# A two-block network on one core: the gates of the second block one stage later, through DRAM, and the experts' end in another order

## The chip, the core and the metric

The kernel runs on one core of a Trainium2 chip. The time is device microseconds of one execution, as the median of several runs. TensorE (PE) does the matrix products, VectorE (DVE), ScalarE (ACT) and GpSimd (POOL) work on elements, and SyncE (SP) issues nearly all loads of weights. Each engine runs its own instructions in order and waits on semaphores for the others.

## The reference

256 tokens of width 1024 pass a first block and then a second one of two layers, all in float32.

```
mod = silu(c) @ ada_w + ada_b                       # first block: 6 vectors of 1024
x = x + g_m * (mixer(norm(x) * (1+sc_m) + sh_m) @ w_out)     # RWKV-7 and mLSTM heads
x = x + g_f * hier_moe(norm(x) * (1+sc_f) + sh_f)            # 32 experts, 2 per token
x = rms_norm(x, final_norm_w)
for layer in 0, 1:                                  # second block
    shift, scale, gate = silu(c_2) @ ada_w_2[layer, 0] + ada_b_2[layer, 0]
    h = norm(x) * (1+scale) + shift
    y = hybrid_attention(h) if layer == 0 else pool_mixer(h)   # pool_mixer ends in * pool_scale
    x = x + gate * y
    shift, scale, gate = silu(c_2) @ ada_w_2[layer, 1] + ada_b_2[layer, 1]
    h = norm(x) * (1+scale) + shift
    x = x + gate * (square(relu(h @ mlp_w1[layer])) @ mlp_w2[layer])
return rms_norm(x, final_norm_w_2)
```

Each expert computes `(silu(x @ w_gate) * (x @ w_up)) @ w_down` with 1024 x 256 weights (256 x 1024 for down), 3 MB per expert. Shift and scale of one of the four sub-blocks of the second block take 8 MB of `ada_w_2`, its gate 4 MB.

## The kernel before

**Weights.** All weights are streamed once, 284 MB in all. SP loads them in pieces of 1 MB into eight slots named `w` (`slot`). For most products ACT casts a piece to a rounded high part `wh` (L293) and DVE subtracts it to get the low part `wl` (L294); the activations are split likewise, and each product is made of three matmuls: high with high, high with low, low with high. The helper `mm` records all of these at L180. Working tiles of 128 x 1024 (`t4`) come from a shared pool of 25; a tile can be taken only when its last user is done. PSUM has seven banks for general use and one for the modulation sums (`pada`).

**Modulation.** The vectors of shift, scale and gate are matrix-vector products whose weights are as large as those of the layers, so they are spread over the whole kernel as side work. There are two lists of side work: list 0 with pieces of products, list 1 with the modulations (`later`). `fill` and `more` take steps from them, `need` finishes one that is due, and the MLP takes up to four steps of list 1 in each of its groups. A step of `ada_steps` loads 1 MB and adds it up on TensorE with eight recorded matmuls (L454). A step of `vector_sum` loads 1 MB and adds it up on DVE in two instructions of 128 x 1024 (L532, L534); after eight steps four matmuls against ones add up over the partitions. `ada_cols` then turns the sums into columns (a DVE copy at L499, four transposes, adds at L505).

**The four gates of the second block.** The two gates of layer 0 are one item (`gates20`), summed together in eight steps during the first block's mixer, and kept as columns. `ada_gate` (by `rows_of`) turns one half of the columns into a row in all partitions: eight matmuls into `pgate` and two ACT copies, once in the attention and once ahead of the first MLP. The two gates of layer 1 are one item too (`gate_rows`), summed in the first MLP, written to DRAM by POOL, and read back into all partitions by two loads on SP each (`gate_load`).

**Order of list 1 in the first block.** `g1`, `f` (its own modulation), `ada00` (shift and scale of the attention), `gates20`, `ada01` (shift and scale of the first MLP). What is left is taken up in the attention.

**Experts.** The loop over `g` takes eight groups of four experts. `quad` multiplies the gathered slots of the four experts by the gate weights and then by the up weights (`pgu`), `act` makes the activation, `down` transposes it (`paT`, L1841), multiplies by the down weights (`pyd`), scales (`mg`, L1856) and splits the result, and `combine` of the group before adds it into `pacc` behind the next gate quad. `behind` holds the instructions of a part until the given instruction is issued. The loads of the expert weights follow in the order of use, as slots come free (`moe_done`). The residual is added to `pacc` as a product with a diagonal matrix (`residual`, `diag`), all eight matmuls at g = 7 ahead of the last `down`.

**Attention bias.** `attn_consts` builds a table of biases. Its last part loads the flipped rows from DRAM (`bflip`, POOL's queue), turns them by two matmuls per tile (`pbf`) and copies them to `bias`; it runs at g = 3 and g = 4. The attention's first weights are queued in `attn_first`, and `warm(W2)` puts six matmuls without use there.

**MLP and wide products.** In `wide_steps`, the first product of the MLP, a piece is used for four output blocks; for each block the high part's products are followed by the low part's.

Of the kernel before, what the change touches and what calls it, by code (L numbers as in the profile page):

```python
# [9 lines left out]
F32 = mybir.dt.float32  # L10
# [9 lines left out]
T = 256  # L20
# [41 lines left out]
W2 = 6  # L62
# [90 lines left out]
class Net:  # L153
# [392 lines left out]
    def gate_rows(self, l, out):  # L546

        nc, I = self.nc, self.I
        p = yield from self.vector_sum(1, [I["ada_w_2"][l, s][:, 2048:3072] for s in range(2)])
        t = self.t4("grow")  # L550
        s, f = t[:, 0:512], t[:, 512:1024]
        for j in range(4):
            nc.gpsimd.dma_start(s[32 * j:32 * j + 32],
                              I["ada_b_2"][l, j // 2:j // 2 + 1, 2048 + 512 * (j % 2):2560 + 512 * (j % 2)].to_broadcast([32, 512]))
        nc.vector.tensor_add(s, s, p)
        if l == 1:
            for j in range(2):
                nc.gpsimd.dma_start(f[32 * j:32 * j + 32], I["pool_scale_2"][:, 512 * j:512 * j + 512].to_broadcast([32, 512]))
            nc.vector.tensor_mul(s[0:64], s[0:64], f[0:64])
        d = out["d"] = self.dpool.tile([4, 512], F32, name=f"gate_d{l}")  # L560
        for j in range(4):
            nc.gpsimd.dma_start(d[j:j + 1], s[32 * j:32 * j + 1])

    def gate_load(self, d, half, name):
        g = self.t4(name)
        for j in range(2):
            r = 2 * half + j
            self.nc.sync.dma_start(g[:, j * 512:(j + 1) * 512], d[r:r + 1].to_broadcast([128, 512]))
# [198 lines left out]
    def wide_steps(self, H, wide, first, evac):  # L767
# [6 lines left out]
        for _ in range(4):  # L774
            for kc, h, l in self.piece():
# [10 lines left out]
                for j in range(4):  # L786
# [4 lines left out]
                    else:  # L791
                        mm(j, h, hh, 0, f)
                        mm(j, h, hl, 1, False)
                    mm(j, l, hh, 0, False)
# [898 lines left out]
    def overflow(self, S, gate, acc):  # L1693
# [5 lines left out]
        with tc.If(fl != 0):  # L1699
            co = mp.tile([128, 2, 32], F32, name="cwo", tag="cwo", bufs=1)  # L1700
            nc.vector.scalar_tensor_tensor(co, pos, CAP - 0.5, cw, op0=ALU.is_gt, op1=ALU.mult)
            cd = self.dpool.tile([32, 128, 2], F32, name="cwo_d")
            nc.gpsimd.dma_start(cd.rearrange("e p a -> p a e"), co, allow_slow_non_contiguous=True)
# [11 lines left out]
            with tc.For_i(0, 32, 1) as e:  # L1715
# [11 lines left out]
                cc = mp.tile([128, 1, 2], F32, name="ccol", tag="occ", bufs=1)  # L1727
                nc.gpsimd.dma_start(cc, cd[bass.ds(e, 1)].rearrange("o p a -> p o a"))
                for a in range(2):
# [10 lines left out]
                    nc.vector.tensor_scalar(act, act, cc[:, 0, a:a + 1], None, op0=ALU.mult)  # L1740
# [76 lines left out]
    def moe(self, S, consts):  # L1817
# [52 lines left out]
        def residual():  # L1870

            d = self.t4("diag")[:, 0:T]
            for a in range(2):
                da = d[:, a * 128:(a + 1) * 128]
                nc.vector.tensor_scalar(da, self.c("ident"), S["sd"][:, a:a + 1], None, op0=ALU.mult)
                for c in range(2):
# [782 lines left out]
```

## Time and profile before

| what | value |
|---|---|
| runs | 1039.04, 1031.16, 1039.94 us, median 1039.04 |
| profiled execution | 1031.61 us, its span 1029.9 |
| mean granted clock of TensorE | 0.978 |
| busy, share of the span | PE 92%, PEld 70%, DVE 56%, ACT 42%, POOL 4% |
| moved | 284.49 MB, mean 276 GB/s |
| instructions | 17630 |

The busy share of an engine is an average over stages that differ much: the first block's mixer lies before 290 us, the experts between 290 and 510, the attention up to 640, the first MLP up to 826, then the pool mixer and the second MLP. A time next to an instruction is its start, counted from the start of the span.

### The profile page before, as it was taken

How to read it: one execution, taken by the hardware profiler on the slowest of the kernel's cores; microseconds unless marked ns; L12 is line 12 of the kernel's file. 1: busy time of each engine (PE TensorE's matmuls, PEld its weight loads, DVE VectorE, ACT ScalarE, POOL GpSimd, SP SyncE). 2: the span in 40 equal slices, each digit the busy share in tenths (PEclk: the TensorE clock that was granted, in tenths of full speed). 3: DMA queues.
4: the chain of work that ended last, by engine and by line, in shares of the span. 5: the costliest groups of instructions: out<-in, count | busy, mean ns of one | idle time of the engine just before them, and what ended most of it. 6: DMA issues, size and time to landing. Idle time of an engine off the chain costs nothing. (4 is left out here: it accounts for less than half of the span.)

```text
span 1029.9 us, 17630 instructions
## 1 busy us (share of the span) xinstructions
PE 948.0 (92%) x7303; PEld 725.8 (70%) x7303; DVE 577.7 (56%) x987; ACT 435.1 (42%) x733; POOL 40.3 (4%) x55
## 2 busy tenths in 40 slices
PE   4899999999998788776989999999999989999996
PEld 2687776687665444433377798988888878888885
DVE  1475744657633221111266648998889776555556
ACT  1373223244332111111257545755555567555663
POOL 1011000010100000000000010010000000000000
PEclk9999999999899999988999999999999999999999
DMA  8989746997789999999977334699989935555501
GB/s 256 342 296 373 287 165 209 346 404 260 260 322 384 411 405 416 416 402 418 381 274 249 107 103 164 242 383 328 345 304 370 331 114 190 185 198 192 176 1 41
DMA packets 88760, 284.49 MB, mean 276 GB/s; under 512 B 10525, under 2 KB 13906, under 8 KB 76774
## 3 DMA queue, kind: packets, MB, share of 16 engines
q1 hardware_dynamic: 86922, 280.31, 73.7%
q0 software_dynamic: 800, 1.57, 0.6%
q10 hardware_dynamic: 956, 1.47, 0.4%
q8 instruction: 58, 0.95, 0.4%
q14 instruction: 24, 0.20, 0.1%
HBM read 282.25 MB, written 1.07 MB: 275 GB/s over the span
## 5 line engine op out<-in xcount | busy, mean ns | idle before, releaser
L180 PE MATMUL pB<-hx,wh 128*128 128x256 f32 (+1 forms) x1222 | 292.3, 323 | 3.1 <-ACT wh L293 1.5
L294 DVE TENSOR_TENSOR wl<-w,wh 128x1024 fp32r<-128x1024 f32 x186 | 225.5, 1221 | 121.5 <-ACT wh L293 118.9
L293 ACT CAST wh<-w 128x1024 fp32r<-128x1024 f32 x186 | 193.8, 1049 | 193.6 <-PE pB L180 101.9
L180 PEld LDWEIGHTS pB<-hx,wh 128*128 128x128 f32 x1222 | 200.6, 190 | 36.1 <-issue 10.7
L180 PE MATMUL pB<-hx,wl 128*128 128x256 f32 x800 | 221.3, 284 | 2.0 <-DVE wl L294 1.9
L180 PEld LDWEIGHTS pB<-hx,wl 128*128 128x128 f32 x800 | 149.9, 190 | 7.2 <-DVE wl L294 3.5
L180 PE MATMUL pgu<-w,xg 128*32 128x256 f32 x848 | 74.4, 439 | 29.7 <-DMA w<-in_moe_w_gate_dram 24.1
L180 PE MATMUL pm<-wh,fh 128*128 128x512 f32 (+1 forms) x262 | 100.9, 388 | 0.0
L180 PE MATMUL pm<-wl,fh 128*128 128x512 f32 (+1 forms) x262 | 100.9, 385 | 0.0
L180 PE MATMUL pm<-wh,fl 128*128 128x512 f32 (+1 forms) x262 | 100.9, 385 | 0.0
L180 PEld LDWEIGHTS pgu<-w,xg 128*32 128x32 f32 x848 | 33.3, 125 | 66.5 <-DMA w<-in_moe_w_gate_dram 32.6
L534 DVE SCALAR_TENSOR_TENSOR w<-w,csil 128x1024 f32<-128x1024 f32 x56 | 70.6, 1286 | 5.2 <-DMA w<-in_ada_w_dram 5.2
L180 PEld LDWEIGHTS pm<-wh,fh 128*128 128x128 f32 x262 | 49.2, 188 | 12.3 <-issue 2.5
L180 PEld LDWEIGHTS pm<-wh,fl 128*128 128x128 f32 x262 | 49.2, 188 | 10.0
L180 PEld LDWEIGHTS pm<-wl,fh 128*128 128x128 f32 x262 | 49.3, 188 | 9.7 <-DVE wl L294 0.4
L1856 DVE SCALAR_TENSOR_TENSOR mg<-pyd,slotw,g_f 128x512 f32<-128x512 f32 x16 | 12.0, 749 | 50.5 <-PE pyd L180 50.5
L1649 DVE TENSOR_TENSOR oh<-cs,pos 128x256 f32<-128x256 f32 x8 | 3.4, 426 | 65.0 <-PE pcw L180 64.9
L454 PE MATMUL pada<-w,csil 128*32 128x512 f32 x256 | 38.3, 603 | 0.0
L180 PE MATMUL pyd<-w,aT 128*32 128x512 f32 x216 | 30.5, 596 | 7.8 <-ACT aT L1843 7.8
L1678 ACT CAST slotT<-pcw 128x256 fp32r<-128x256 f32 x8 | 3.0, 373 | 80.0 <-PE pcw L180 80.0
L180 PEld LDWEIGHTS pxg<-oh,xp 128*128 128x128 f32 x256 | 29.2, 192 | 3.0 <-issue 2.5
L180 PE MATMUL pxg<-oh,xp 128*128 128x128 f32 x256 | 30.6, 278 | 0.1
(547 smaller groups left out, 1287.8 us busy)
## 6 DMA issues: line engine op xcount, KB each, us to landing
w<-in_mlp_w_dram SPq DMA_DIRECT2D x64, 1024.0 KB
w<-in_ada_w_dram SPq DMA_DIRECT2D x40, 1024.0 KB
w<-in_ada_w_dram SPq DMA_DIRECT2D x64, 512.0 KB
w<-in_moe_w_up_dram SPq DMA_DIRECT2D x28, 1024.0 KB
w<-in_moe_w_down_dram SPq DMA_DIRECT2D x26, 1024.0 KB
w<-in_moe_w_gate_dram SPq DMA_DIRECT2D x25, 1024.0 KB
w<-in_w_in_dram SPq DMA_DIRECT2D x12, 1024.0 KB
w<-in_attn_w_in_dram SPq DMA_DIRECT2D x9, 1024.0 KB
```

Source lines behind the costliest of these rows:

```text
L180: return self.nc.tensor.matmul(out, lhsT, rhs, **kw)
L293: nc.scalar.copy(h, w)
L294: self.split_ins = nc.vector.tensor_sub(l, w, h)
L454: nc.tensor.matmul(acc[32 * j:32 * j + 32, :], self.csil[:, which, k:k + 1].to_broadcast([128, 32]), w[:, j * 512:(j + 1) * 512], start=(k ...
L534: nc.vector.scalar_tensor_tensor(acc[:, s], w[:, s], ck, acc[:, s], op0=ALU.mult, op1=ALU.add)
L1649: nc.vector.tensor_tensor(oh.rearrange("p a (e s) -> p a e s", s=32), self.c("slots")[:, None, None, :].to_broadcast([128, 2, 4, 32]), S[" ...
L1678: nc.scalar.copy(ot, p[:, 0:T])
L1856: nc.vector.scalar_tensor_tensor(yg[:, s], py[c], cwg, gate[:, s], op0=ALU.mult, op1=ALU.mult)
```

## The change

1. The gates of the second block are four items `g00`, `g01`, `g10`, `g11`. Each sums one gate alone (`gate_row`, four loads of 1 MB that hold two parts each, two matmuls against ones), adds the bias, and writes two rows to DRAM by POOL. `gate_load` reads them back on SP. `g00` stands in the place of `gates20`; `g10` and `g01` are summed in the first MLP, `g11` in the second. `pool_scale` goes into `g10` alone.
2. `ada01` joins list 1 only after `route`; two steps of list 1 are taken ahead of the last `combine`.
3. The residual is added in halves, at g = 5 and g = 6, behind the gate quad. The loads of `bflip` move to SP's queue at g = 7; their products and copies come behind `attn_first`, and `W2` is 2.
4. In `wide_steps` the low part's products of all four blocks follow the high part's.
5. In the path for overflowing experts (a branch that isn't taken with these inputs) a table in DRAM has another layout.

```diff
-    def gate_rows(self, l, out):
+    def gate_row(self, l, h, out):
-        p = yield from self.vector_sum(1, [I["ada_w_2"][l, s][:, 2048:3072] for s in range(2)])
+        v = I["ada_w_2"][l, h][:, 2048:3072].rearrange("(p j) n -> p j n", j=8)
+        acc = None
+        for k in range(0, 8, 2):
+            w = self.slot()
+            nc.sync.dma_start(w.rearrange("p (j n) -> p j n", j=2), v[:, k:k + 2])
+            self.small_loads()
+            self.used(False)
+            for j in range(2):
+                x, ck = w[:, j * 1024:(j + 1) * 1024], self.csil[:, 1, k + j:k + j + 1]
+                if acc is None:
+                    acc = x
+                    nc.vector.tensor_scalar(acc, x, ck, None, op0=ALU.mult)
+                else:
+                    nc.vector.scalar_tensor_tensor(acc, x, ck, acc, op0=ALU.mult, op1=ALU.add)
+            yield 2.9
+        p = self.ps("pada", "ada")
         t = self.t4("grow")
+        s, f = t[0:64, 0:512], t[0:64, 512:1024]
+        for j in range(2):
+            q = slice(32 * j, 32 * j + 32)
+            self.mm(p[q], self.ones[:, 0:32], acc[:, j * 512:(j + 1) * 512], start=True, stop=True)
+            nc.gpsimd.dma_start(s[q], I["ada_b_2"][l, h:h + 1, 2048 + 512 * j:2560 + 512 * j].to_broadcast([32, 512]))
+        nc.vector.tensor_add(s, s, p[0:64])
...
+        d = out["d"] = self.dpool.tile([2, 512], F32, name=f"gate_d{l}{h}")
+        for j in range(2):
             nc.gpsimd.dma_start(d[j:j + 1], s[32 * j:32 * j + 1])
...
+                for j in range(4):
                     mm(j, l, hh, 0, False)
...
+        def residual(a):
+            d = self.t1("diag")[:, 0:128]
+            nc.vector.tensor_scalar(d, self.c("ident"), S["sd"][:, a:a + 1], None, op0=ALU.mult)
...
+                if g in (5, 6):
+                    residual(g - 5)
+                if g == 7:
+                    next(consts)
...
-                if g in (3, 4):
-                    next(consts)
-                if g == 7:
-                    residual()
                 last = ot, *down(g, t, cwg)
+        self.more(2)
         combine(7, *last)
...
+            nc.sync.dma_start(f.rearrange("p (h k) -> p h k", h=4), src)
...
-        self.ada2_gates(0, "gates20", A["g20"])
-        self.ada2(0, 1, "ada01", A["01"])
+        self.ada2_gate(0, 0, "g00", A["g00"])
...
+        self.ada2(0, 1, "ada01", A["01"])
         acc, fw, fw2 = self.moe(R, consts)
...
         self.attn_first(*((n, (u_ins, sq_ins), (n[0], sq_ins), (n0, sq_ins))[E5]))
+        next(consts)
...
-        self.gate = self.ada_gate(A["g20"]["m"], 0, "g00")
+        self.gate = self.gate_load(A["g00"]["d"], "g00")
...
-        with self.behind(*self.half_ins[1][1:1 + G1]):
-            self.gate = self.ada_gate(A["g20"]["m"], 1, "g01")
...
-        self.later("gates21", self.gate_rows(1, A["g21"]), lane=1)
+        self.ada2_gate(1, 0, "g10", A["g10"])
+        self.ada2_gate(0, 1, "g01", A["g01"])
         self.ada2(1, 1, "ada11", A["11"])
         def last():
-            self.need("ada10", "gates21")
+            self.need("ada10", "g10", "g01")
+            self.gate = self.gate_load(A["g01"]["d"], "g01")
...
-        self.gate = self.gate_load(A["g21"]["d"], 1, "g11")
...
-        self.mlp(H, ss, 4, lambda: None)
+        self.ada2_gate(1, 1, "g11", A["g11"])
+        def last():
+            self.need("g11")
+            self.gate = self.gate_load(A["g11"]["d"], "g11")
+        self.mlp(H, ss, 4, last)
```

## Rows read from the trace of the kernel before

**Rows 1.** Windows: length, busy us (count) of PE PEld DVE ACT POOL, PEclk, DMA share, GB/s.

```profile
230.00:290.00 60.00, 54.78 (x305) 40.79 (x305) 41.92 (x105) 24.14 (x44) 5.95 (x10) 0.94 0.75 271
297.00:499.00 202.00, 163.22 (x1579) 93.29 (x1576) 40.69 (x99) 33.25 (x75) 1.65 (x2) 0.92 1.00 403
499.00:516.00 17.00, 13.89 (x56) 4.75 (x54) 6.54 (x19) 5.68 (x14) 1.41 (x2) 1.00 1.01 376
640.00:840.00 200.00, 197.54 (x1180) 172.28 (x1178) 171.50 (x203) 112.92 (x166) 6.65 (x13) 1.00 0.86 311
```

**Rows 2.** Timeline, DVE, 248 to 264: start, length, instruction, count, [idle before, releaser].

```profile
248.66 2.55 DVE L534 SCALAR_TENSOR_TENSOR w<-w,csil 128x1024 f32<-128x1024 f32 x2 [1.58 <-DMA w<-in_ada_w_dram]
...
262.72 1.28 DVE L534 SCALAR_TENSOR_TENSOR w<-w,csil 128x1024 f32<-128x1024 f32 x1
```

**Rows 3.** Timeline, PE, 248 to 290.

```profile
248.60 1.12 PE L180 MATMUL pgb<-arow,cs 4*128 4x256 f32 x4
...
264.32 1.92 PE L180 MATMUL pada<-w,one 128*32 128x512 f32 x4
...
284.32 1.92 PE L454 MATMUL pada<-w,csil 128*32 128x512 f32 x16
```

**Rows 4.** Two windows in which the granted clock was low.

```profile
260.30:267.00 6.70, 6.36 (x18) 2.98 (x16) 4.97 (x8) 1.24 (x2) 0.09 (x1) 0.50 0.83 301
355.90:362.60 6.70, 5.53 (x52) 2.57 (x56) 0.00 (x0) 0.00 (x0) 0.00 (x0) 0.50 1.01 422
```

**Rows 5.** Page, part 6, and timeline of POOL: the loads of the bias.

```profile
bflip<-brow_d POOLq DMA_DIRECT2D x2, 512.0 KB, 9.9
...
332.20 0.90 POOL L1962 DMA_DIRECT2D bflip<-brow_d  x1 [45.48 <-ACT mh L1857]
```

**Rows 6.** Timeline, PE, one mid expert group and the last.

```profile
374.27 1.88 PE L180 MATMUL pbf<-bflip,cs 128*128 128x512 f32 x4
...
397.12 3.64 PE L180 MATMUL pgu<-w,xg 128*32 128x256 f32 x58 [1.76 <-DMA w<-in_moe_w_up_dram]
...
489.28 3.64 PE L180 MATMUL pgu<-w,xg 128*32 128x256 f32 x58 [1.86 <-DMA w<-in_moe_w_up_dram]
492.85 7.16 PE L180 MATMUL pacc<-xp,diag 128*128 128x512 f32 x8
499.83 0.40 PE L1841 MATMUL paT<-cs,actm 128*128 128x128 f32 x2
...
508.81 0.74 PE L180 MATMUL pacc<-mh,slotT 128*128 128x512 f32 x2
```

**Rows 7.** Timeline, DVE, the last group.

```profile
493.83 0.42 DVE L1835 TENSOR_TENSOR actm<-actm,pgu 128x256 f32<-128x256 f32 x1
507.20 0.75 DVE L1856 SCALAR_TENSOR_TENSOR mg<-pyd,slotw,g_f 128x512 f32<-128x512 f32 x1 [12.95 <-PE pyd L180]
```

**Rows 8.** Timeline, SP, 480 to 610: DMA issues.

```profile
485.31 1.12 SPq L1785 DMA_DIRECT2D w<-in_moe_w_down_dram  x2
492.53 7.15 SPq L719 DMA_DIRECT2D w<-in_attn_w_in_dram  x4
508.07 1.29 SPq L442 DMA_DIRECT2D w<-in_ada_w_dram  x3
...
553.25 6.42 SPq L719 DMA_DIRECT2D w<-in_attn_w_out_dram  x4
```

**Rows 9.** The chain of waits, attention and first MLP.

```profile
590.50 1.78 PE pgate L180 x16
...
709.53 0.99 PE pada L180 x8
```

**Rows 10.** Timeline, PE: first product with the attention's output weights.

```profile
614.41 0.40 PE L180 MATMUL po<-wh,yh 128*128 128x512 f32 x1
```

**Rows 11.** Windows of one group of each MLP; columns as in the first group.

```profile
662.00:684.00 22.00, 22.00 (x128) 19.38 (x128) 21.64 (x22) 12.15 (x16) 3.05 (x6) 1.00 0.98 377
862.00:884.30 22.30, 22.30 (x115) 18.94 (x114) 12.70 (x15) 12.79 (x18) 0.00 (x0) 1.00 0.61 195
```

More of the change, by code (lines that the diff above doesn't have):

```diff
@@ L557, in gate_rows, with gate_load @@
             for j in range(2):
                 nc.gpsimd.dma_start(f[32 * j:32 * j + 32], I["pool_scale_2"][:, 512 * j:512 * j + 512].to_broadcast([32, 512]))
-            nc.vector.tensor_mul(s[0:64], s[0:64], f[0:64])
-        d = out["d"] = self.dpool.tile([4, 512], F32, name=f"gate_d{l}")
-        for j in range(4):
+            nc.vector.tensor_mul(s, s, f)
+        d = out["d"] = self.dpool.tile([2, 512], F32, name=f"gate_d{l}{h}")
+        for j in range(2):
             nc.gpsimd.dma_start(d[j:j + 1], s[32 * j:32 * j + 1])
-    def gate_load(self, d, half, name):
+    def gate_load(self, d, name):
@@ L1868, in combine @@
                     self.mm(acc[a, c], o, yl[:, s], start=False, stop=(g == 7))
[L1870 to L1876, printed above, removed]
-                    self.mm(acc[a, c], da, S["xp"][a].rearrange("t (j p) -> t p j", j=8)[:, 64 * c:64 * c + 64],
-                            start=False, stop=False)
+        def residual(a):
+            d = self.t1("diag")[:, 0:128]
+            nc.vector.tensor_scalar(d, self.c("ident"), S["sd"][:, a:a + 1], None, op0=ALU.mult)
+            for c in range(2):
+                self.mm(acc[a, c], d, S["xp"][a].rearrange("t (j p) -> t p j", j=8)[:, 64 * c:64 * c + 64],
+                        start=False, stop=False)
         last = None
@@ L1957, in attn_consts @@
         yield
-        self.bias = []
-        for i in range(2):
-            f = self.t4("bflip")
+        F = [self.t4("bflip") for _ in range(2)]
+        for i, f in enumerate(F):
             src = bass.AP(tensor=brow.tensor, offset=brow.offset + 4 * i * 384, ap=[[1, 128], [384, 4], [1, 256]])
-            nc.gpsimd.dma_start(f.rearrange("p (h k) -> p h k", h=4), src)
-            t = self.t4("bias")
+            nc.sync.dma_start(f.rearrange("p (h k) -> p h k", h=4), src)
+        yield
+        self.bias = [self.t4("bias") for _ in range(2)]
+        for f, t in zip(F, self.bias):
             for j in range(2):
@@ L1967, in attn_consts @@
                 nc.scalar.copy(t[:, j * 512:(j + 1) * 512], p)
-            self.bias.append(t)
-            yield
+        yield
     def attn_first(self, *ins):
@@ L2402, in ada2, with ada2_gate @@
         self.later(name, steps(), lane=1)
-    def ada2_gates(self, l, name, out):
-        r = 12 + 12 * l + 4
-        srcs = [self.I["ada_w_2"][l, s][:, 2048:3072] for s in range(2)]
-        self.later(name, self.ada_vector(1, srcs, [r, r + 6], name, out), lane=1)
+    def ada2_gate(self, l, h, name, out):
+        self.later(name, self.gate_row(l, h, out), lane=1)
     def run(self):
         nc, I = self.nc, self.I
-        A = {n: {} for n in ("m", "g1", "f", "00", "g20", "01", "10", "g21", "11")}
+        A = {n: {} for n in ("m", "g1", "f", "00", "g00", "01", "g01", "10", "g10", "11", "g11")}
         self.setup()
@@ L2564, in run @@
         self.dump("os", osw)
-        self.need("gqk", "gv", "gates20")
-        self.gate = self.ada_gate(A["g20"]["m"], 0, "g00")
+        self.need("gqk", "gv", "g00")
+        self.gate = self.gate_load(A["g00"]["d"], "g00")
         HH = [None, self.split_act(osw)]
```

24 lines of the change are left out of this document (9 added, 15 removed).

## The prediction, made before the changed kernel was timed

> **What bounds the kernel now.** I read the windows by stage first, since the span's averages mix stages with different limits. Three kinds of stage are to be seen in [rows 1]. From 297 to 499 us, the experts, the DMA share is 1.00 at 403 GB/s while TensorE is busy for 163 of 202 us: bytes set the end there. From 640 to 840, the first MLP, TensorE is busy for 197.5 of 200: products set the end. From 230 to 290 and from 499 to 516 neither is full, and the end is set by chains of small steps. Then the timelines of the two mixed stretches show what each chain waits for: VectorE and TensorE around 248 to 290 [rows 2, 3], and the last expert group [rows 6, 7] with SP's issues around it [rows 8]. The chain of waits [rows 9] says which small pieces in the later stages lie on the path.
>
> The sum is made against the profiled execution, 1031.61 us (span 1029.9, 1.7 around it). The median of the three runs shown, 1039.04, lies 7.4 above it; two of the runs are near the median and one is near the profiled one. The difference is put on the median unchanged.
>
> **The change, part by part.**
>
> *Front, 230 to 290.* The summed gates of layer 0 had 8 load steps, and the last two are the VectorE pairs of 2.55 us (two of 1.28) that run between the mixer's own steps. The pair at 248.66 ends at 251.2, while the product pgb that the next mixer step reads was done at 249.72 [rows 2, 3]: 1.4 us too late. The sum at 264.32 takes 1.92 us of TensorE (low clock, [rows 4]) ahead of the mixer's output products [rows 3]. Both go: -3.3. The new g00 has four steps, all earlier, and one sum of its own there; a sum costs 0.99 on the chain [rows 9], so +0.9 in a stretch full of products. Two steps of ada01 (16 matmuls, 1.92 us at 284.32) leave a stretch in which TensorE was waiting for the route; nothing for that. POOL gets four small DMAs for g00, 0.9 us each by the issue in [rows 5], with POOL busy for 6 of 60 us [rows 1]: 0, at most +3.6. Front: **-2.4** (-3.3 to +1.2).
>
> *Bias loads out of the expert stream.* Two loads of 512 KB, 1.05 MB, were issued at 332 in POOL's queue [rows 5], inside the full stream. At 403 GB/s they cost 1.05/0.403 = 2.6 us of it, and they now come behind the last down weights. The stream starts when the first gate products free slots, which the change doesn't touch, so its end comes **-2.6** earlier (0 if other transfers fill in). The loads showed 9.9 us from issue to landing [rows 5], so in POOL's queue they seem to have stood among the weights rather than gone past them. The Trainium skill (DMA: Bandwidth & Descriptors, section Queues, rings and completion order) says that a DMA engine takes turns between the queue rows that have work. By it the loads on SP's row now hold up everything that SP issues after them, which speaks against the move; the second rival has that as a mechanism.
>
> *Residual off the tail.* Eight matmuls, 7.16 us, stand between the last up products and the transposes of the activation [rows 6]. The activation was ready at 494.25 and the transposes started at 499.83 [rows 6, 7]: 5.6 us. What is late next is the last down load. The last up weights were waited for until 489.28; four down loads, 4.19 MB at 0.403 MB/us, take 10.4 us, so the last lands at 499.7 (less 2.6 by the step above, as everything in this stage). If expert 31 held up all the down products the gain would be about 1.0; if nothing did, 7.2. Three of four experts have landed before, so I take 0.75 x 5.6 = **-4.2**. The residual's halves now stand behind the gate quads of groups 5 and 6, 3.6 us each; each up quad starts with a DMA wait (1.76 at 397.12, [rows 6]) and the down weights behind it are queued far ahead, so 0 (at most +1.8 each if not covered).
>
> *Bias products at the attention's start.* Twice 1.88 us [rows 6] = 3.76 leave waits for DMA, where they were free, and come to the end of the tail, where TensorE is idle for 17.00 - 13.89 = 3.1 us [rows 1]; four warming matmuls go, which ran in idle time. **+0.7** (0 to +3.8). The two steps of ada01 before the last combine: two loads, 16 matmuls, 1.92 us at [rows 3]'s rate, mostly in the wait for the scaled outputs (mg at 507.20, combine at 508.81, [rows 6, 7]): **+0.5** (0 to +3.9, second rival).
>
> *Attention.* The gate's broadcast products, 1.78 us on the chain at 590.50 [rows 9], go: **-1.8**. The second set of these ran in the norm's gap: 0. In their place are two row loads on SP, priced in the fourth rival.
>
> *MLPs.* Before, the first MLP had one sum for both gates of layer 1; now it has two, and the second MLP one. A sum is 0.99 on the chain [rows 9], with half the matmuls perhaps 0.5: **+1.7** (+1.0 to +2.0). Bytes move from one MLP to the other: 24 MB of modulation in the first either way (28 steps against 27), 4 MB more in the second. VectorE is at 21.64 of 22.00 us in a group of the first, and at 12.70 of 22.30 in one of the second, where four steps of 2.55 bring it to 22.9 [rows 11, 2]: **+0.3** (0 to +2).
>
> *Reordered wide products.* The same matmuls; the TensorE idle time they could touch is 200 - 197.5 = 2.5 us in the first MLP [rows 1]: 0 (-1 to +1). The overflow path isn't taken: 0.
>
> Sum: -2.4 - 2.6 - 4.2 + 0.7 + 0.5 - 1.8 + 1.7 + 0.3 = **-7.8**. From the profiled execution that is 1023.8, from the median **1031.2**.
>
> **Rivals.**
> *One, nothing follows the residual:* down products start as soon as the activation is there, -7.2 instead of -4.2, 1028.2. For it: pieces of 0.43 us can fill in as weights land. Against: the landing worked out above.
> *Two, the combine stands behind ada01:* if TensorE has those 16 matmuls ahead of the last combine, it waits for their loads. Last down at 497.1, bias 1.05 MB more to 499.7, two ada loads 2.1 MB to 504.9, one more microsecond for the products: 505.9, against a combine at 508.81 - 2.6 - 4.2 = 502.0. That eats 3.9, less the 0.5 already counted: 1034.6. For it: the three ada loads at 508.07 were issued at once when slots came free [rows 8]. Against: matmuls without their data may be put later.
> *Three, the clock:* the granted clock was 0.50, 1.2 of 2.4 GHz, for 6.7 us twice, once inside the expert stage, where TensorE waits for weights [rows 4]. Without the residual's 7 us TensorE has a wait just before the down products. One more such stretch costs half of it, 3.35: 1034.6. The Trainium skill (TensorE: Matmul & The Clock Gate, section HAM oscillation) describes waits for DMA between bursts of matmuls that let the clock fall each time; the stretch at 355.90 agrees, the tail of before, at 1.00, shows none.
> *Four, slower, SP blocked:* the row load of g00 waits on SP for a free buffer, and whatever SP issues behind it waits too. The attention's output weights were issued at 553.25 [rows 8] and first used at 614.41 [rows 10]. Four loads take 10.4 us, so it decides from a release later than 604.0; held until the first use it costs 10.4, 1041.6. For it: the products that made the old gate ran only at 590.50 [rows 9], so a buffer may not be free long before. Against: fifty microseconds of room.
> *Five, the order stays:* the scheduler leaves residual and bias about where they were, and the stream's and the tail's 6.8 are not gained: 1038.0.
>
> **Numbers.** Chances: forecast 0.45, one 0.10, two 0.20, three 0.10, four 0.08, five 0.07. A measurement of this kernel can tell about 1% from no change: under 1028.6 is faster, over 1049.4 slower. The forecast is 0.75% faster, so about 0.37 for faster: rival one, and the part of the forecast in which the runs lie by the profiled one (one of three did), or the bounds fall well. Slower needs rival four together with the upper bounds: 0.07. The rest, 0.56, is the same. The range goes from 1020.0 (the 1023.8 of the profiled execution with rival one's 3.0 and some bounds) to 1038.5 (rival five).
>
> **What would show it.** A first output product ahead of which no pada stands (front); no bias load between 297 and 499, and the last up quad waiting until about 484 (489.28 - 2.4 - 2.6); the transposes of the last group right behind its activation; the combine not behind a pada that waits for DMA; no pgate on the chain; MLP groups at their old lengths. It would be wrong if the time from the end of the last up quad to the last combine, 16.0 us now [rows 6], came out over 14 instead of 11.8, if a low clock showed after 490, or if SP stood still before the output weights.

## The result, and the profile after

Over 20 runs each the changed kernel took 1043.28 us (1034.15 to 1057.03) and the kernel before 1037.01 (1029.01 to 1049.33): ratio **1.0065 [1.0039, 1.0092]**, 0.65% slower where 0.75% faster was forecast. The profiled executions are 1035.09 (span 1033.4) and 1031.61: +3.5, where the sum said -7.8. Ratios and mean clocks are of fast runs: a run more than 1.5% above the fastest of its kernel, such as the 1057.03 here or the profiled one of b_gates below, is left out. The changed kernel's profile flatters it: its mean granted clock, 0.977, is the highest of its runs (0.955 to 0.977, mean 0.9645). The kernel before, run beside every experiment, has 0.9733 in 125 runs.

Windows of the changed kernel: first the stretches of [rows 1] and [rows 11], then those in which its clock was low (answering to [rows 4]).

```profile
230.00:290.00 60.00, 51.60 (x277) 42.37 (x277) 35.67 (x93) 24.84 (x45) 7.04 (x12) 0.88 0.73 277
297.00:499.00 202.00, 162.54 (x1631) 92.92 (x1624) 40.96 (x99) 32.14 (x74) 0.00 (x0) 0.96 0.97 392
499.00:516.00 17.00, 15.06 (x81) 7.13 (x79) 10.45 (x28) 9.60 (x23) 1.40 (x2) 1.00 1.05 384
640.00:840.00 200.00, 196.62 (x1149) 171.12 (x1148) 167.69 (x193) 110.21 (x157) 6.20 (x12) 0.98 0.86 311
862.00:884.30 22.30, 22.30 (x115) 18.99 (x114) 19.28 (x22) 14.62 (x22) 0.00 (x0) 1.00 0.88 307
...
241.00:245.00 4.00, 4.00 (x16) 2.92 (x15) 2.41 (x6) 1.04 (x2) 0.00 (x0) 0.57 1.04 411
285.50:293.00 7.50, 4.52 (x18) 4.13 (x19) 4.20 (x30) 1.23 (x6) 0.43 (x2) 0.54 0.66 270
828.50:835.50 7.00, 7.00 (x36) 7.00 (x35) 3.33 (x4) 2.96 (x5) 0.00 (x0) 0.51 0.40 122
```

The seventh column is the granted clock. It is 0.88 and 0.98 where before had 0.94 and 1.00, and the last three rows say where: in the mixer, in the wait for the route, and in the pool mixer. A fourth stretch at half clock, 3.4 us from 599.9, stands in the attention. The mixer's old one, 6.8 us around 260 [rows 4], is there in both kernels (from 262.0 in the changed one). In the experts the changed kernel has less of it, 17 us against 31, but there the bytes set the end.

Timeline of TensorE in the changed kernel, answering to [rows 3, 6].

```profile
219.02 1.04 PE L180 MATMUL pada<-w,one 128*32 128x512 f32 x2
219.99 1.05 PE L180 MATMUL phs<-cs,ysq 128*128 128x2 f32 x8
220.98 1.04 PE L180 MATMUL pada<-w,one 128*32 128x512 f32 x2
...
238.94 0.28 PE L1380 MATMUL pgc<-cs,arow 4*128 4x4 f32 x2 [0.62 <-DVE arow L1373]
240.42 1.10 PE L180 MATMUL pgb<-arow,cs 4*128 4x256 f32 x4 [1.20 <-DVE gm L1382]
241.44 1.66 PE L180 MATMUL psc<-qk 64*128 64x256 f32 x8
...
261.86 2.08 PE L433 MATMUL pbc<-cs,rb 128*128 128x128 f32 x8 [2.10 <-DVE rb L428]
...
282.81 1.84 PE L180 MATMUL plg<-wgr,hT 128*128 128x36 f32 x15
288.48 0.64 PE L180 MATMUL ppos<-Bm,cs 128*128 128x32 f32 x2 [3.83 <-DVE Bm L1630]
...
291.64 4.24 PE L180 MATMUL pxg<-oh,xp 128*128 128x128 f32 x32
...
490.03 3.64 PE L180 MATMUL pgu<-w,xg 128*32 128x256 f32 x58 [1.41 <-DMA w<-in_moe_w_up_dram]
495.14 0.41 PE L1857 MATMUL paT<-cs,actm 128*128 128x128 f32 x2 [1.47 <-DVE actm L1851]
...
502.81 0.72 PE L180 MATMUL pacc<-mh,slotT 128*128 128x512 f32 x2
...
507.52 1.06 PE L454 MATMUL pada<-w,csil 128*32 128x512 f32 x8
510.04 1.12 PE L180 MATMUL pbf<-bflip,cs 128*128 128x512 f32 x2 [1.45 <-ACT xn L2556]
...
826.93 8.66 PE L180 MATMUL pwin<-band,xn 128*128 128x16 f32 x46 [3.17 <-DVE xn L643]
```

The same places in the kernel before:

```profile
258.00 1.05 PE L180 MATMUL pada<-w,one 128*32 128x512 f32 x4
260.00 2.08 PE L433 MATMUL pbc<-cs,rb 128*128 128x128 f32 x8 [0.96 <-DVE rb L428]
...
287.77 0.41 PE L180 MATMUL ppos<-Bm,cs 128*128 128x32 f32 x2 [1.53 <-DVE Bm L1614]
...
827.37 5.62 PE L180 MATMUL pwin<-band,xn 128*128 128x16 f32 x48 [1.29 <-DVE xn L628]
```

Read from the end: the pool mixer's first products (pwin) waited 3.17 us for VectorE and then took 8.66; before they took 5.62 behind a wait of 1.29. Ahead of ppos, the small products of the route, stands a wait of 3.83; before it was 1.53, behind the 16 pada of [rows 3]. The tail did what was forecast and more: from the end of the last up products, 493.67, to the last combine, 502.81, are 9.1 us (16.0 before, 11.8 forecast).

VectorE and SP in the changed kernel, answering to [rows 7] and [rows 8].

```profile
494.58 0.42 DVE L1851 TENSOR_TENSOR actm<-actm,pgu 128x256 f32<-128x256 f32 x1
...
813.89 2.35 DVE L2611 TENSOR_TENSOR w<-w,g 128x1024 f32<-128x1024 f32 x2
816.16 3.49 DVE L294 TENSOR_TENSOR wl<-w,wh 128x1024 fp32r<-128x1024 f32 x3
819.57 1.01 DVE L1475 TENSOR_TENSOR res<-pm,g 128x256 f32<-128x256 f32 x2
```

```profile
487.85 5.92 SPq L1976 DMA_DIRECT2D bflip<-brow_d  x2
493.86 3.49 SPq L442 DMA_DIRECT2D w<-in_ada_w_dram  x2
497.44 10.92 SPq L734 DMA_DIRECT2D w<-in_attn_w_in_dram  x4
...
580.96 0.97 SPq L583 DMA_DIRECT2D g<-gate_d  x2
```

SP issued the row load of g00 at 580.96, when all loads of the attention's output weights had been issued (from 550.95 on); it blocked none of them.

The chain of waits, answering to [rows 9].

```profile
587.91 0.91 PE pga L180 x30
...
590.45 0.44 PE pgk L2106 x4
...
730.24 0.98 PE pada L180 x4
753.57 0.98 PE pada L180 x4
...
894.99 0.98 PE pada L180 x4
```

No pgate stands between pga and pgk, and the three new gates' sums take 0.98 each.

Lengths of the stages in single profiled executions, in us, by first or last matmuls of TensorE's timeline (mixer: first `po` to `plg`; route: to the first `pgu`; experts: to the last `pgu`; tail: to `pgl`; attention: to its last `po`; MLP 1: to its last `pm`; wait: to `pwin`; pool: to the last `ppl`; MLP 2: to its last `pm`). The last column is the mean granted clock of the kernel's timed runs.

| kernel | mixer | route | experts | tail | attention | MLP 1 | wait | pool | MLP 2 | clock |
|---|---|---|---|---|---|---|---|---|---|---|
| before | 47.98 | 15.41 | 199.45 | 25.87 | 118.63 | 187.75 | 2.21 | 11.60 | 182.91 | 0.9733 |
| after | 48.12 | 17.03 | 197.86 | 20.94 | 119.94 | 188.28 | 4.10 | 15.10 | 183.25 | 0.9645 |
| b_g0 | 46.69 | 16.73 | 198.11 | 25.87 | 121.50 | 193.67 | 4.21 | 16.22 | 182.97 | 0.9695 |
| b_ada01 | 47.95 | 18.00 | 198.45 | 25.82 | 123.46 | 187.75 | 2.21 | 11.62 | 182.84 | 0.9706 |
| b_end | 47.90 | 15.40 | 196.91 | 20.12 | 121.82 | 187.76 | 2.21 | 11.61 | 182.85 | 0.9742 |
| b_wide | 51.70 | 15.41 | 198.63 | 25.87 | 118.62 | 186.72 | 2.89 | 16.68 | 182.11 | 0.9692 |
| a_g20 | 49.79 | 18.03 | 198.09 | 20.96 | 121.68 | 186.92 | 4.06 | 15.09 | 183.19 | 0.9658 |
| a_nowide | 48.09 | 17.07 | 198.83 | 22.55 | 121.44 | 189.33 | 2.79 | 15.10 | 185.69 | 0.9638 |
| a_warm2 | 47.48 | 15.41 | 197.48 | 22.58 | 119.89 | 188.32 | 4.07 | 11.84 | 183.25 | 0.9766 |
| best2 | 51.70 | 15.40 | 197.40 | 21.37 | 118.11 | 187.74 | 2.22 | 11.60 | 182.95 | 0.9747 |

The mixer's length scatters by up to 4 us between executions without any edit there: in b_wide and best2 its clock was at 0.50 for 17 us in place of the 6.8 of before, and it took 51.7. So a single profile is weak for it. With g00 in the first block the scatter is wider: four of nine profiles (a_ada01, a_all, a_last, a_warm) have one stretch of 20.5 us at 0.50, from between 250 and 257 on, and mixers of 52.3 to 58.1; none of ten without g00 there has one. The profile of after has none either.

The account between the two profiles, after minus before: up to 211 us -2.2 (ahead of anything changed, scatter); from there to the first output product +2.7, which holds g00's sum of 2.1; mixer +0.1; route +1.6; experts -1.6; tail -4.9; attention +1.3; MLP 1 +0.5; wait +1.9; pool +3.5; MLP 2 and end +0.4. Together +3.3 as rounded (the spans: +3.5).

### The profile page after: what moved, and what is told of

It reads as the page before. It is cut to its first block, busy times and chain, and to the rows that moved or that the text cites. A ratio compares the mean times of both kernels' runs of the same rounds, so it can differ in the third digit from the quotient of the medians.

```text
span 1033.4 us, 17587 instructions
## 1 busy us (share of the span) xinstructions
PE 944.6 (91%) x7263; PEld 725.7 (70%) x7263; DVE 578.8 (56%) x987; ACT 432.5 (42%) x729; POOL 42.0 (4%) x61
## 4 chain that ended last, share of the span: by engine, by line
PE 45%; DVE 3%; ACT 1%; DMA 1%; issue 1%; POOL 0%; POOLq 0%; ACTq 0%
PE pB L180 21%; PE pm L180 16%; PE po L180 2%; PE pgv L180 1%; PE pwin L180 1%; DMA w<-in_ada_w_dram 1%; DVE x L1476 1%; PE pso L180 1%; PE pada L180 0%; DVE res L1475 0%; PE pss L180 0%; PE ppl L180 0%; DVE wl L294 0%; PE pgo L180 0%; ACT wh L293 0%
## 5 line engine op out<-in xcount | busy, mean ns | idle before, releaser
L180 PE MATMUL pB<-hx,wh 128*128 128x256 f32 (+1 forms) x1222 | 249.6, 321 | 3.6 <-ACT wh L293 1.5
L180 PEld LDWEIGHTS pB<-hx,wh 128*128 128x128 f32 x1222 | 191.9, 190 | 32.7 <-issue 12.7
L180 PE MATMUL pB<-hx,wl 128*128 128x256 f32 x800 | 160.5, 284 | 1.2 <-DVE wl L294 1.2
L180 PEld LDWEIGHTS pB<-hx,wl 128*128 128x128 f32 x800 | 127.7, 190 | 10.2 <-issue 2.3
L180 PE MATMUL pgu<-w,xg 128*32 128x256 f32 x848 | 70.9, 426 | 26.6 <-DMA w<-in_moe_w_gate_dram 18.9
```

Source lines behind the costliest of these rows:

```text
L180: return self.nc.tensor.matmul(out, lhsT, rhs, **kw)
```

## The experiments

**Theory A:** the tail gains as forecast; the loss is the clock, which falls where side work used to fill short waits of TensorE, now moved away or finished early. **Rival B:** the loss is one piece of added work, above all g00's sum in the first block. The times are ratios to the kernel before on the same chip, with 95% intervals.

### One part at a time

`b_end`, before with part 3 alone:

```diff
+                if g in (5, 6):
+                    residual(g - 5)
...
+            nc.sync.dma_start(f.rearrange("p (h k) -> p h k", h=4), src)
...
+        next(consts)          # behind attn_first; W2 = 2
```

> The kernel before with only the experts' end of the change: residual in halves at groups 5 and 6, bias loads on SP at group 7, their products behind attn_first, W2 = 2; gates and ada01 as before. In the changed kernel's trace the time from the end of the last up quad to the last combine fell from 16.0 to 9.2 us. Theory A (the clock: the changed kernel loses where TensorE has lost the side work that kept it busy; low-clock stretches were added at 241, 286, 600 and 828) and theory B (side work moved onto the path: g00's sum in the mixer's norm, six steps of ada01 in the full attention, one more sum per MLP) both say that this part alone keeps its gain: -6 at the combine, -2 to -3 more or less for the stream, in all 5 to 8 us faster than before, ratio 0.992 to 0.995. If the tail's gain is itself lost again in the attention (its weights come later), the ratio is 0.998 to 1.001.

**0.995 [0.9917, 0.9982]**, 1030.29 us. The tail is 5.75 shorter, the experts 2.5, but the attention 3.2 longer. TensorE's timeline in b_end:

```profile
505.21 1.13 PE L180 MATMUL pbf<-bflip,cs 128*128 128x512 f32 x2 [2.53 <-DVE xn L2540]
...
506.96 1.91 PE L643 MATMUL ptr<-cs,xn 128*128 128x128 f32 x16
...
517.01 0.39 PE L180 MATMUL pB<-hx,wl 128*128 128x256 f32 x1 [2.16 <-DVE wl L294]
```

The last bias tile waits for VectorE's norm and stands ahead of the transposes (ptr) that need the same norm; then comes a wait of 2.16 with a low clock behind it (517.6 to 521).

`b_gates`, before with part 1 alone: 

> The kernel before with only the gates of the change (four single sums, rows through DRAM); ada01 stays queued in the first block, the experts' end as before. Theory A: ada01's steps are still there for the route's wait, so no low clock at 286 to 293, but the pool mixer's low-clock stretch (about 3 us) comes if it hangs on the first MLP's end. Ratio 1.000 to 1.004. Theory B: +2.1 us for g00's sum, +0.8 for the MLPs, -1.8 for the attention's gate products, -1.9 for the old sum: -1 to +1 us, ratio 0.999 to 1.001.

**1.0094 [1.0053, 1.0135]**, 1046.0. Its halves are `b_g0` (layer 0's gates; g01's 4 MB come on top of the old pair of layer 1 in the first MLP) and `b_g1` (layer 1's):

```diff
-        self.ada2_gates(0, "gates20", A["g20"])       # b_g0
+        self.ada2_gate(0, 0, "g00", A["g00"])
-        self.later("gates21", self.gate_rows(1, A["g21"]), lane=1)   # b_g1
+        self.ada2_gate(1, 0, "g10", A["g10"])
```

> The kernel before with only layer 0's gates changed: g00 alone in the first block, its row through DRAM, g01 in the first MLP; layer 1's gates, ada01 and the experts' end as before. The trace of the gates-only kernel shows low-clock stretches at 242 to 249 and 255 to 276 in the first block's mixer, where the kernel before has one at 260 to 267. Theory A1 (the loss of the gates is in the first block: g00's bias row holds VectorE for 1.3 us ahead of the mixer's small chain, TensorE waits there and its clock falls): ratio 1.006 to 1.011, about the whole loss of the gates-only kernel (1.0094). Theory A2 (the loss is in the MLPs and the pool mixer): ratio 0.998 to 1.002.

> The kernel before with only layer 1's gates changed: g10 in the first MLP, g11 in the second, each summed alone; the rest as before. Theory A1: the first MLP loses four steps, the second gains four: ratio 0.999 to 1.002. Theory A2: ratio 1.005 to 1.009, with the pool mixer's low-clock stretch.

b_g0: **1.0109 [1.0059, 1.0159]**, with 4 MB too much in the first MLP (193.67 for 187.75, so 0.57 of its 1.09%), so not clean. b_g1: **0.9978 [0.9942, 1.0013]**, no loss. Part 1's loss is layer 0's; where in layer 0's half it lies, these two don't say.

`b_ada01`, before with part 2 alone:

```diff
+        self.more(2)                                   # ahead of the last combine
-        self.ada2(0, 1, "ada01", A["01"])              # list 1, ahead of route
+        self.ada2(0, 1, "ada01", A["01"])              # behind route
```

> The kernel before with ada01 alone moved behind the route, and two of its steps ahead of the last combine (part 2). Theory: the route's wait is empty, a low clock shows between 286 and 297 and the route takes 17 to 18 us in place of 15.4; in the attention more sums of ada01, 2 to 3 us: ratio 1.002 to 1.005. Rival (ada01 has to be summed somewhere, and costs the same in either place): 0.999 to 1.001.

**1.0055 [1.0028, 1.0083]**, 1039.94: in the route, Theory A's mechanism without g00. Timeline and window of b_ada01, then the same window of before:

```profile
286.93 0.64 PE L180 MATMUL ppos<-Bm,cs 128*128 128x32 f32 x2 [3.37 <-DVE Bm L1614]
...
290.09 5.20 PE L180 MATMUL pxg<-oh,xp 128*128 128x128 f32 x32
```

```profile
284.00:297.00 13.00, 10.07 (x78) 8.88 (x82) 5.51 (x34) 2.68 (x10) 0.43 (x2) 0.74 0.44 174
```

```profile
284.00:297.00 13.00, 11.38 (x126) 7.54 (x124) 6.31 (x39) 3.55 (x10) 0.43 (x2) 1.00 0.75 292
```

The call that takes three steps of list 1 in the route's wait (`self.more(R3)`) finds the list empty. The wait is bare, the clock is at half of 2.4 GHz from 286.3 to 293.1, and the route takes 18.0 in place of 15.4. The attention is 4.8 longer, though it holds no more of ada01's sums: 48 recorded matmuls from its first `pgl` to its last `po` in both kernels, and the two steps taken ahead of the last combine come before it. It is TensorE's waits that grew, 3.6 us against 1.6, the longest for VectorE's wl (1.92 at 528.60), and a clock at 0.50 from 528.7 for 3.4 us came with them. A likely reason, not tested: SP issued the two ada01 loads at 493.28, ahead of the attention's first four weights, whose issue then ended at 509.7 in place of 499.7.

`b_wide`, before with part 4 alone (the added loop `for j in range(4)`): 

> The kernel before with part 4 alone (in wide_steps the low part's products of all four blocks behind the high part's). Theory: TensorE ends the first MLP about 1.0 us earlier but waits longer ahead of the pool mixer (2.2 us before, 3 to 4 expected), the granted clock falls to 0.50 there and the pool mixer takes about 15 us in place of 11.6: ratio 1.001 to 1.004. Rival: the order is free, the lengths stay 187.8, 2.2 and 11.6: ratio 0.998 to 1.000.

**1.0015 [0.9981, 1.0048]**: no difference clear of the noise. MLP 1 is 1.0 shorter, as expected, but the pool mixer is 5.1 longer. Timeline of b_wide:

```profile
830.55 9.84 PE L180 MATMUL pwin<-band,xn 128*128 128x16 f32 x46 [1.97 <-DVE xn L628]
```

TensorE ends earlier, VectorE doesn't; the wait is 2.89 in place of 2.21, and the clock is low from 831.0 to 841.2.

The parts alone add up to +0.94 + 0.55 - 0.50 + 0.15 = +1.14%; together they give +0.65%. With four intervals of 0.3 to 0.4 on the parts, that difference isn't clear of the noise. Two overlaps would go that way: parts 1 and 2 both lengthen the route (by 1.3 in b_g0, at full clock, and 2.6 in b_ada01; by 1.6 together), and parts 1 and 4 each drop the clock in the same pool mixer, which can be lost only once.

### One part undone

`a_ada01` (after, ada01 back in the first block, no steps ahead of the last combine), `a_g20` (after, layer 0's gates as before), `a_g00late` (after, g00 queued behind the route, ahead of ada01), `a_nowide` (after without part 4):

```diff
+        self.ada2(0, 1, "ada01", A["01"])              # a_ada01: ahead of route; more(2) removed
+        self.ada2_gates(0, "gates20", A["g20"])        # a_g20: in g00's place
-        self.ada2_gate(0, 0, "g00", A["g00"])          # a_g00late: moved behind route
-                for j in range(4):                     # a_nowide
```

> The changed kernel with ada01 queued in the first block again, behind g00, and no steps taken ahead of the last combine. Theory A: the route's wait is filled again, the first gate quad comes 1.6 us earlier, and fewer steps are left for the attention: 3 to 5 us faster than the changed kernel, ratio to before about 1.002. Theory B alone (no clock): 2.6 us faster by the steps out of the attention, less what the first block then pays for them.

> The changed kernel with layer 0's gates as before: summed together in the first block, turned into rows by products; everything else stays changed (ada01 behind the route, the experts' end, layer 1's single sums, the order of the wide products). Theory A1 (g00 in the first block costs some 7 us there on average: three of six profiles with it had a low-clock stretch of 20 us from 255 on, none of six without): the mixer has only the stretch at 260, the pool mixer has none; only the route's wait still lets the clock fall. Ratio to before 0.994 to 0.999. Rival: the first block's loss comes from ada01's absence or lies outside it: ratio 1.003 to 1.007.

> The changed kernel with g00 queued behind the route too, ahead of ada01: the first block then has neither old nor new gate of layer 0, nor VectorE's add of g00's bias, and the attention takes four steps more. If g00's own instructions (a sum of 2 us, a bias add that holds VectorE 1.3 us) are what lets the clock fall in the mixer: no wait of 0.62 us ahead of pgc, no low-clock stretch at 241 and none of 20 us from 255 on; the first gate quad 3 to 8 us earlier than in the changed kernel's slow profiles. If it is that the old steps and sums are missing as fill: the long stretch is there without g00 as well, and TensorE's 2.1 us wait ahead of pbc stays. Ratio 0.998 to 1.003 in the first case, 1.005 to 1.010 in the second.

> The changed kernel without part 4. Theory (part 4 helps the clock fall ahead of the pool mixer): the first MLP about 1.0 us longer, the wait behind it 4.1 to about 2.8, the pool mixer 15.1 to between 11.6 and 15: ratio 1.003 to 1.006. Rival (part 4 is free): as the changed kernel, 1.006 to 1.007.

They measured **1.0077 [1.0041, 1.0113]**, **1.0057 [1.0024, 1.0089]**, **1.0109 [1.0065, 1.0153]** and **1.009 [1.0061, 1.0119]**. Undoing one part alone brings nothing back. That ends rival B for the changed kernel: without g00 in the first block (a_g20, a_g00late) the loss stays. The stretch at half clock at 242 stands in these two as well, so it isn't g00's. Nor is part 4 to blame in the changed kernel: without it MLP 1 is 1.05 longer, the wait 1.3 shorter, and the pool mixer's 15.1 stays. The pool mixer's low clock has two causes that are each enough, part 4 (b_wide) and part 1: a_nowide has it without part 4, b_g0 with layer 0's gates alone, and parts 2 and 3 alone leave it at 11.6.

### Filling the waits, and nothing else

`a_warm` puts matmuls without use into the route's wait and ahead of the pool mixer; `a_warm2` also into the mixer; `b_warm` is the control, the same in the kernel before, which has its sums in the route's wait still:

```diff
-W1 = 4
+W1 = 16                      # ahead of the pool mixer
+        self.warm(3)         # a_warm2, b_warm: ahead of pgc
+        self.warm(6)         # a_warm2, b_warm: ahead of pgb
-        self.more(R3)
+        self.warm(14)        # a_warm, a_warm2: the route's wait
```

> The changed kernel with 14 warming matmuls (no use for the result) in the route's wait, in place of the empty call for three steps, and 16 instead of 4 ahead of the pool mixer. Nothing else moves. Theory A: the clock stays at 1.00 from 286 to 293 and from 828 to 835, the first gate quad comes 1.6 us earlier and the pool mixer is 3.0 us shorter: 4.6 us faster than the changed kernel, ratio to before about 1.002. Theory B: no change against the changed kernel, ratio about 1.0065.

> The changed kernel with the warming matmuls of the earlier run (route's wait, pool mixer) and nine more at the mixer's two small waits around 239 to 241 us. Theory A1: TensorE keeps its clock from 241 on, the first block ends 2 to 10 us earlier: ratio to before 0.990 to 0.996. If the clock there falls for what comes later (the products on few columns at 245 to 260), the stretches at 255 stay: ratio 0.998 to 1.000 as without them.

> Control: the kernel before with the same warming matmuls in the mixer (nine) and ahead of the pool mixer (16 instead of 4); the route's wait keeps its three steps of ada01. In its trace neither place has a low-clock stretch, only 260 to 267 behind the mixer. If the warming matmuls give back only what the change lost (theory A), this kernel is within 0.3% of before: 0.997 to 1.003. If they help any kernel of this kind, 0.992 to 0.996.

a_warm **0.9995 [0.9963, 1.0027]**, a_warm2 **0.9954 [0.9918, 0.9989]**, b_warm **1.0016 [0.9987, 1.0045]**. Timeline and windows of a_warm2:

```profile
285.95 3.46 PE L224 MATMUL pwarm<-ident_r 128*128 128x512 f32 x14
289.97 0.41 PE L180 MATMUL ppos<-Bm,cs 128*128 128x32 f32 x2 [0.56 <-DVE Bm L1632]
...
828.00 5.40 PE L180 MATMUL pwin<-band,xn 128*128 128x16 f32 x46 [0.39 <-DVE xn L643]
```

```profile
284.00:297.00 13.00, 12.35 (x101) 10.23 (x103) 7.05 (x38) 4.28 (x10) 1.75 (x4) 1.00 0.60 236
826.00:842.00 16.00, 13.80 (x108) 12.73 (x107) 11.48 (x27) 9.75 (x23) 1.98 (x4) 1.00 0.26 93
241.00:245.00 4.00, 4.00 (x22) 2.78 (x22) 2.38 (x8) 1.15 (x3) 0.22 (x1) 1.00 1.03 409
```

The wait ahead of the pool mixer is as long as in after (4.07 against 4.10), but filled; the three stretches are at 1.00, the route is back to 15.41 and the pool mixer to 11.84. Work that computes nothing makes the changed kernel 1.1% faster and the old one no faster. The other profiles agree: in the seven with a bare wait in the route (after, a_bias, a_g00late, a_g20, a_last, a_nowide, b_ada01) it takes 16.9 to 18.5 at a low clock, in the three with fillers there (a_warm, a_warm2, a_all) 15.4; the pool mixer takes 13.2 to 16.5 in the seven variants of the changed kernel without fillers, 11.6 to 11.8 in these three. This shows the second half of theory A for the kernel as a whole: what it loses against before is the clock in unfilled waits. It doesn't show that filling is all that counts: in b_warm's profile the clock fell for 3.4 us from 289.8, behind the wait that has its sums, and a_all's mixer has the long stretch in spite of its nine fillers.

`a_bias` (g00's bias rows loaded before its sum), `a_last` (g01's row load behind g10's), `a_all` (a_warm2 with a_last, W1 = 8) tried smaller suspects:

> The changed kernel with the bias rows of each gate loaded when its first weights are, not after its sum. VectorE's add of g00's bias then doesn't wait for POOL's load (0.66 us in the changed kernel's trace) ahead of the mixer's small chain. If that wait is what lets TensorE's clock fall at 241, those stretches go and the kernel gains 2 to 10 us, ratio to before 0.997 to 1.004; if the add itself (0.68 us) and the sum are enough, nothing changes: ratio 1.006.

> The changed kernel with one pair of loads moved: the row load of g01 comes behind that of g10, so the pool weights' product with g10 stands one place earlier on VectorE, as before. Theory A: TensorE's wait ahead of the pool mixer falls from 3.2 to about 1.3 us, the clock stays at 1.00 there, and 3 to 5 us come back: ratio to before 1.002 to 1.004, and no low-clock stretch between 825 and 845. If the wait hangs on something else, 1.006 and the stretch stays.

> The changed kernel with the warming matmuls in the mixer and in the route's wait, g01's row load behind g10's, and 8 warming matmuls ahead of the pool mixer. Theory A: as the kernel with all warming matmuls (0.9954) or 1 to 2 us better: 0.993 to 0.996.

a_bias **1.0017 [0.9985, 1.0049]** and a_last **1.0021 [0.9982, 1.0059]** lie below the changed kernel's 1.0065, but the intervals overlap, and their profiles still have the long route (18.5, 18.4): unsettled. a_bias took the wait ahead of pgc from 0.62 to 0.20, and the low stretch behind it stayed (3.4 us from 241.6). a_last took the wait ahead of pwin from 4.1 to 2.8 and the pool mixer from 15.1 to 13.2; its low stretch there is half as long and not gone. a_all **0.9966 [0.9938, 0.9995]** is no better than a_warm2.

### A version that beats both

`best1` is b_end with layer 1's gates; `best2` is b_end with the bias products behind ptr and `W2` left at 6:

```diff
-        next(consts)          # behind attn_first
...
+        next(consts)          # behind the attention's first norm is turned
```

> The kernel before with the experts' end of the change and the single sums of layer 1's gates (g10 in the first MLP, g11 in the second); layer 0's gates and ada01 stay as before. The two alone gave 0.995 and 0.998. Theory A: they touch different stages and add up: 0.991 to 0.995. If the tail's gain falls away where less side work is left, 0.996 to 1.000.

> The kernel before with the experts' end of part 3 (as in the run b_end, 0.995), but the bias products placed behind the attention's first norm has been turned (ptr), and six warming matmuls kept. Theory: in b_end the last bias tile waits 2.5 us for VectorE's norm and stands ahead of ptr, so ptr comes about 1.75 us earlier here, and the bias fills the 2.2 us wait for the first wl: ratio 0.990 to 0.994. Rival (VectorE, which copies the bias, sets the start): as b_end, 0.995, or worse.

best1 **0.9976 [0.9946, 1.0006]**: layer 1's gates add nothing. best2 **0.9942 [0.9915, 0.9969]**, 1029.22 us, the lowest ratio of all. TensorE's timeline in best2:

```profile
512.05 1.94 PE L643 MATMUL ptr<-cs,xn 128*128 128x128 f32 x16 [1.28 <-DVE xn L2540]
513.83 3.60 PE L180 MATMUL pbf<-bflip,cs 128*128 128x512 f32 x8
516.86 1.61 PE L180 MATMUL pgl<-hx,wglr 128*32 128x256 f32 x9
```

The bias now fills the time in which hx and wl are made. Tail and attention together take 139.5 us, against 141.9 in b_end and 144.5 before. Its interval overlaps b_end's: that best2 beats b_end is seen in this stage of one profile each, and not shown by the time.

## Why the prediction was wrong, step by step

**The front (-2.4) failed, by two terms.** "Two steps of ada01 (16 matmuls, 1.92 us at 284.32) leave a stretch in which TensorE was waiting for the route; nothing for that": the sums were the filling of that wait. Without them the clock fell to half and the route took 1.6 more in after, 2.6 in b_ada01; all of part 2 costs 0.55% of 1035 alone, 5.7 us (2.9 to 8.6), the rest of it at the attention's start. And "+0.9 in a stretch full of products" for g00's sum: it fell among the norm's own small products (pada at 219.02 and 220.98 around phs), twice 1.04 us because phs parted its two halves, and that stretch grew by 2.7. With layer 0's gates in this form part 1 alone costs 0.94%, more than part 2; no run says how much of that is the sum.

The gain of 3.3 was mis-sized. The 1.4 for the last VectorE pair is how late the pair ended, not how long TensorE waited: it had other products, and idled 0.42 ahead of psc, the mixer's small products behind pgb. From the first output product to pbc the changed kernel is 1.3 longer, with psc and what follows at half clock from 241.5. The pada at 258.00 is gone, but it stood in a wait for VectorE that is now bare (2.10 ahead of pbc, 0.96 before). From pbc to plg it is 1.15 shorter: that is the sum at 264.32, priced at 1.92. So the mixer stayed at 48. The wait ahead of pgb was 1.20 before too, and the low clock behind it is also in three kernels whose mixer nobody changed (b_g1, b_wide, best2), so that stretch isn't shown to come from the change.

**The expert stream (-2.6)** isn't shown. It is -1.6 in after and -2.5 in b_end; but over all profiles the stage takes 198.1 to 200.6 in six with the bias loads in POOL's queue and 196.9 to 200.6 in thirteen with them on SP, 0.5 apart in the mean. The prediction's own sign failed: the last up quad was to wait until about 484, and waited until 490.03. The Trainium skill (DMA: Bandwidth & Descriptors, section Queues, rings and completion order) says that a DMA engine takes turns between the queue rows that have work, from which the prediction took its objection to the move. In b_end the tail gained all the same; whether the loads held up the attention's first weights (+3.2 there) no run separates.

**The tail (-4.2 + 0.7 + 0.5 = -3.0)** was right in mechanism and mis-sized: -4.9. The transposes started 0.14 behind the activation's end, so the landing of the last down load held up nothing: that is rival one, given 0.10. Rival two is out: the combine at 502.81 stands ahead of the pada at 507.52. Part of this gain went back at the attention's start, where the last pbf waited for the norm; the 0.7 for the bias products assumed idle time that VectorE's norm had to end first.

**The attention (-1.8)** was right about pgate, and came out at +1.3. TensorE is busy for 116.9 us of it (117.0 before, with pgate), so something else took pgate's place, and its waits are 3.0 in place of 1.6. In it are the 3.4 us at half clock from 599.9 (half of that is 1.7) and waits at its start, 1.69 for VectorE at 526.49 the longest. The forecast had no term for what parts 2 and 3 put ahead of the attention; each alone made it longer (4.8 and 3.2).

**The MLPs (+2.0)** came out at +0.5 and +0.3 inside. Part 4 alone took 1.0 and 0.8 off them (b_wide), so the sums and the moved bytes cost about 2.7: three sums of 0.98 in place of one of 0.99 are 2.0 of it, where the forecast had 1.7 (half the matmuls were priced at half the time). Between the MLPs the forecast was wrong, by +5.4 in the wait and the pool mixer. The term for the reordered wide products, 0, looked only at TensorE's idle time; the order makes TensorE finish before VectorE, whose chain (w by g, three wl, res at 819.57) ended no earlier (res at 819.87 before).

**Rival three, the clock**, was the right kind in the wrong place, and one stretch at 3.35 where there were four (3.4, 6.8, 3.4 and 6.8 us at half clock). I looked at the tail, where the wait ends on a DMA. The Trainium skill (TensorE: Matmul & The Clock Gate, HAM oscillation) describes waits for DMA; here the waits ahead of ppos and pwin end on VectorE [3.83, 3.17 above], and the clock fell all the same.

**Rivals four and five** didn't happen. The range missed by 4.8 us; its upper end was rival five, in which the stream's and the tail's gains don't come, although three unknowns (clock, sums in new places, order) could each cost.

That the clock carries nearly all of the measured loss is a second reading, by numbers of all runs and not by an experiment: over 125 runs of the kernel before, time and mean granted clock go together (correlation -0.93) at 8.6 us per 0.01, in the changed kernel at 7.1. Its clock is 0.0088 lower: an estimate of 6.2 to 7.6 us, against 0.65% of 1037, 6.7. By the same reckoning a_warm2 owes 3.7 of the 4.8 us by which it beats before to a clock 0.0043 above that of before on its chip. So at an equal clock the changed kernel would be about as fast as the old one, and the forecast gain of 7.8 isn't there: the gains of tail and pgate would be paid for by g00's sum, the attention's start and the MLPs. For the parts alone the clock carries less: the means differ by 0.0042 in b_gates and 0.0015 in b_ada01, 3.6 of 9.7 and 1.3 of 5.7 us.

**Open:** what the rest of these two losses is; which low stretches the changed kernel has at its mean clock of 0.9645, since only an execution at 0.977 was profiled, and whether the mixer's long one is among them; and why b_wide and best2 have two low stretches more in a mixer with nothing changed.

## What to carry to other kernels

Before moving side work out of a wait, write down what the wait is then filled with: "TensorE was waiting anyway" is a price of zero only if the clock holds without it. When products are made to end earlier, look at which engine ends last at the next hand-over; if it is another one, the gain becomes a wait. A load or a sum that is moved ahead of a stage belongs into that stage's term. And compare the clock of the profiled execution with that of all runs, and a stage's length over several profiles, before reading a sum from one.

## What the runs showed of the hardware that I had not expected

- TensorE fell to half clock behind waits on VectorE in which it was not quite idle: four pwarm stand in the wait ahead of pwin, 4.10 us in after and 2.89 in b_wide, while before kept its clock behind 2.21. pwin took 8.66 and 9.84 us at the low clock, 5.62 and 5.40 at full clock. In a_warm2, with 14 matmuls of 3.46 us in all in the route's wait, the clock stayed at 1.00 there.
- A gate's sum took 0.98 us when its four recorded matmuls stood together (753.57), and the old sum of eight 0.99 [rows 9]; parted into two pairs it took 1.04 for each pair (219.02, 220.98). The halves write different partitions of the result, and where they stood together the trace has them start within 0.01 us of each other, so they seem to run side by side.
- All 138 runs of the unchanged kernel lie between 1028.5 and 1052.2 us, 2.3% apart, on four chips, and the mean granted clock of each run follows its time (correlation -0.96).
